# A down-projection with early row splits at its start and a written order on four engines in its second half

## The chip, the cores and the metric

The kernel runs on one core of a Trainium2 chip. The metric is the device time of one execution in microseconds (us). The work of a core is shared by TensorE (PE, the matrix engine), VectorE (DVE), ScalarE (ACT), GpSimd (POOL) and SyncE (SP, which issues the loads and stores). Each engine works through its own list of instructions in a fixed order, and semaphores make an instruction wait for results of other engines.

## The reference, cut to what matters

The program is one transformer-like layer: a mixer with two kinds of recurrent heads, and then a feed-forward part with a 3x3 depthwise convolution. Only the end of the feed-forward part and the final norm are touched here:

```python
def _conv_ffn(h, w_up, conv_w, w_down, rows, cols):
    u = _dwconv2d(h @ w_up, conv_w, rows, cols)
    a, b = jnp.split(u, 2, axis=-1)
    return (jax.nn.silu(a) * b) @ w_down
...
        xl = xl + g2 * _conv_ffn(_modulate(_rmsnorm(xl, norm2_w[l]), sh2, sc2), w_up[l], ffn_conv_w[l],
                                 w_down[l], rows, GRID_W)
...
    return _rmsnorm(xl, final_norm_w)
```

There are 1024 tokens and 1024 model columns; the hidden width D_FF is 2816, which is 22 blocks of 128.

## The kernel before, in words

**Three products for one.** Every matrix product is done on split operands: a float32 array x becomes a rounded part xh (a cast, on ACT) and a rest xl = x - xh (a subtraction, on DVE or POOL), and PE adds up xh*wh, xh*wl and xl*wh. So each operand needs a cast and a subtraction before PE can use it.

**Up-projection (lines 1504 to 1586).** For each of the 22 blocks j, PE makes two column blocks of the hidden layer (j and 22 + j) from `low` (the normalised input, split, in 16 tiles with the tags L0 to L15, two tags for each of the eight blocks k of the model width). ACT starts each convolution with the middle tap, DVE adds the other eight taps (line 1524), each a SCALAR_TENSOR_TENSOR on the result of the one before it. ACT applies silu (L1582), POOL multiplies the two halves (L1586) into the tile G[j]. For the last block, j = 21, the two products are first copied out of PSUM into `src` tiles (L1565), so that the down-projection can have the PSUM.

**Down-projection (lines 1598 to 1667).** It runs in two halves, `dh` = 0 and 1, of 512 output columns. In each half PE goes over the 22 blocks c of the hidden width; one step c is 24 matmuls (8 token tiles t by 3 products, in `mm`, L1609), and the eight 128x512 results fill all of PSUM. `down_ops` (L1533) prepares a step: the cast and rest of the weight row (wh L1554 on ACT, wl L1555 on POOL, in four buffers each), and the cast and rest of G[c] (gh L1556 on ACT, gl L1557 on DVE, or on POOL for c < 3 of the first half). The trace names both tiles of the row `gd`; the one of c = 0 is named gh and gl. The row tiles take over the tags of `low`: step c uses L0 and L1 if c is even, L2 and L3 if odd, so the row of step c + 2 can be made only when PE is done with step c. In the second half the last four blocks (18 to 21, `rest`) are prepared into tiles of their own and are multiplied last, with the token tile as the outer loop, so that the token tiles are finished one after the other.

**Between the halves.** `evac` (L1629) takes the eight results out of PSUM on DVE, times g2. `acc` adds them to the residual y (L1634, DVE) and sums the squares of the new y (L1636, ACT). POOL then multiplies y by the weight of the final norm (L1645). At the end `final` (L1647) makes the factor 1/rms with three small POOL operations, scales the two halves of a token tile (ACT L1652, DVE L1653) and stores the tile with one transfer of 512 KB (SP).

**What sets the order.** Instructions of an engine that is under `manual_schedule` keep the order in which the program issues them. For the other engines a planner at build time simulates the program with its own costs, places an instruction when it finds it ready, and prefers the one that the program issues earlier. Neither order changes at run time: an instruction that waits holds up all behind it on its engine. During the up-projection no engine is under manual order, during the down-projection PE is, and from line 1657 on PE and DVE.

Of the kernel before, what the change touches and what calls it, by code (L numbers as in the profile page):

```python
# [9 lines left out]
F32 = mybir.dt.float32  # L10
F32R = mybir.dt.float32r
I32 = mybir.dt.int32
AF = mybir.ActivationFunctionType
ALU = mybir.AluOpType
# [3 lines left out]
P = 128  # L18
D = 1024
KD = D // P  # L20
T = 1024
# [3 lines left out]
NLT = T // P  # L25
# [43 lines left out]
WARM = 4  # L69
NL = 4  # L70
NGL = 9
MOVE = ((0, 1, 2, 3), (4, 5, 6, 7))


@with_exitstack
def kernel(ctx: ExitStack, tc: tile.TileContext, A: dict, out: bass.AP):
# [15 lines left out]
    def take(units, n):  # L92
        for _ in range(n):
            next(units, None)

    def raw(ap):
        return ap.bitcast(F32)
# [1398 lines left out]
    with ExitStack() as es:  # L1496
        fp = es.enter_context(pool("ff", bufs=2, side="left"))
        f1 = es.enter_context(pool("ff1", bufs=1, side="left"))
        bt = big_tile(2, "bt")
        bcast_cols(g2bc, mod2[:, 3 * KD:4 * KD], (bt[:, 0:512], bt[:, 512:1024]))  # L1500
        fcw = f1.tile([P, 2 * NF, 9], F32, name="fcw")
        SY.dma_start(out=fcw, in_=A["ffcw"].rearrange("p (a b) -> p a b", b=9))

        def up(ct):
            j, b = ct % NF, ct // NF
            if j == 0:
                return early[b][0]
            halves = split_weights(A["wup"][ct])
            pl = big_tile(2 * j + b, "pu")
            for g in range(2):  # L1510
                up_half(pl, halves, g)
            return pl

        def conv2(acc, src, wcol):
            a3 = acc.rearrange("p (r c) -> p r c", c=GW)
            s3 = src.rearrange("p (r c) -> p r c", c=GW)
            S.activation(acc, src, AF.Copy, scale=wcol(4))  # L1517
            for dy in (0, -1, 1):
                for dx in (-1, 0, 1):
                    if dy == 0 and dx == 0:  # L1520
                        continue
                    r0, r1 = max(0, -dy), GH - max(0, dy)
                    c0, c1 = max(0, -dx), GW - max(0, dx)
                    V.scalar_tensor_tensor(  # L1524
                        a3[:, r0:r1, c0:c1], s3[:, r0 + dy:r1 + dy, c0 + dx:c1 + dx],
                        wcol((dy + 1) * 3 + dx + 1), a3[:, r0:r1, c0:c1], op0=ALU.mult, op1=ALU.add)

        pst = {}

        def g_pool(j):  # L1530
            return Gp if j < NGL else Gr

        def down_ops(c, dh, kind):  # L1533
            if c % 2 == 0:
                st = wp.tile([P, 2, 512], F32, name="wst", bufs=3)
                SY.dma_start(out=st, in_=A["wdown"][dh, c // 2].rearrange("p (a b) -> p a b", a=2))
                pst["s"] = st
                if kind == 2:
                    pst["w"] = [g_pool(c - NF + NL + i).tile([P, 2, 512], F32R, name="wd", tag=f"G{c - NF + NL + i}")
                                for i in range(2)]  # L1540
            src = pst["s"][:, c % 2, :]
            if kind == 2:
                wh, wl = [w[:, c % 2, :] for w in pst["w"]]
                gh, gl = [g_pool(j).tile([P, T], F32R, name="gd", tag=f"G{j}")
                          for j in range(NL + 2 * (c - NF + NL), NL + 2 * (c - NF + NL) + 2)]
            else:
                wh = wp.tile([P, 512], F32R, name="wh", bufs=4)
                wl = wp.tile([P, 512], F32R, name="wl", bufs=4)
                if kind:
                    gh, gl = [lo.tile([P, T], F32R, name="gd", tag=f"L{2 * (c % 2) + i}") for i in range(2)]  # L1550
                else:
                    gh = Gr.tile([P, T], F32R, name="gh")
                    gl = Gr.tile([P, T], F32R, name="gl")
            S.copy(wh, src)  # L1554
            G.tensor_tensor(wl, src, raw(wh), op=ALU.subtract)  # L1555
            S.copy(gh, Gt[c])  # L1556
            (G if dh == 0 and c < 3 else V).tensor_tensor(gl, Gt[c], raw(gh), op=ALU.subtract)  # L1557
            return gh, gl, wh, wl

        def up_src(ct, last):  # L1560
            pl = up(ct)
            if not last:
                return pl
            src = fp.tile([P, T], F32, name="src", tag="cb")
            S.copy(src, pl)  # L1565
            return src

        for j in range(NF):
            if j < len(MOVE):
                for k in MOVE[j]:  # L1570
                    SY.dma_start(out=raw(low[0][k]), in_=raw(h2h[k]))
                    SY.dma_start(out=raw(low[1][k]), in_=raw(h2l[k]))
            if j == len(MOVE) + 1:
                h2h[:], h2l[:] = low
                h2_cm.__exit__(None, None, None)
                Gr = ctx.enter_context(pool("Gr", side="right"))
                Gt.extend(Gr.tile([P, T], F32, name=f"G{i}") for i in range(NGL, NF))
            if j == NF - 1:
                pre0 = down_ops(0, 0, 0)
            pl = up_src(j, j == NF - 1)  # L1580
            conv2(Gt[j], pl, lambda i: fcw[:, j, i:i + 1])
            S.activation(Gt[j], Gt[j], AF.Silu)  # L1582
            pl = up_src(NF + j, j == NF - 1)
            cb = fp.tile([P, T], F32, name="cb", tag="cb")
            conv2(cb, pl, lambda i: fcw[:, NF + j, i:i + 1])
            G.tensor_tensor(Gt[j], Gt[j], cb, op=ALU.mult)  # L1586


# [4 lines left out]
    ms_cm = tc.manual_schedule(engines={mybir.EngineType.PE})  # L1593
    ms_cm.__enter__()
    ys = [lo.tile([P, D], F32, name=f"y{t}", tag=f"L{4 + t}") for t in range(NLT)]
    s0 = d1.tile([P, NLT, 2], F32, name="s0")
    pre = [pre0]
    for dh in range(2):
        ds_ = slice(dh * 512, (dh + 1) * 512)
        pp = [big_tile(i, "pd") for i in range(NLT // 2)]  # L1600
# [2 lines left out]
        def part(c, last, dh=dh):  # L1603
            return down_ops(c, dh, 2 if last else 1)

        def mm(t, c, gh, gl, wh, wl):
            ts_ = slice(t * P, (t + 1) * P)
            for pi, (x, w) in enumerate(((gh, wh), (gh, wl), (gl, wh))):
                PE.matmul(po[t], x[:, ts_], w,  # L1609
                          start=(c == 0 and pi == 0), stop=(c == NF - 1 and pi == 2))  # L1610

        n = NF - NL * dh
        for c in range(n):
            if dh == 0 and 6 <= c < 6 + NLT:
                SY.dma_start(out=ys[c - 6], in_=x1d[c - 6])
            ops = pre.pop(0) if pre else part(c, False)
            for t in (0, 4, 1, 5, 2, 6, 3, 7):
                mm(t, c, *ops)
        rest = [part(c, True) for c in range(n, NF)]

        yt = []
# [2 lines left out]
        def evac(t):  # L1624
            if not yt:
                pair = lo.tile([P, T], F32, name="ytmp", tag=f"L{next(slots)}")
                yt.extend((pair[:, 0:512], pair[:, 512:1024]))
            tmp = yt.pop(0)
            V.tensor_tensor(tmp, po[t], g2bc[:, ds_], op=ALU.mult)  # L1629
            return tmp  # L1630

        def acc(t, tmp):
            y = ys[t][:, ds_]
            V.tensor_tensor(y, y, tmp, op=ALU.add)  # L1634
            sq = dn_.tile([P, 512], F32, name="fsq")
            S.activation(sq, y, AF.Square, accum_out=s0[:, t, dh:dh + 1])  # L1636
            return y

        if dh == 0:
            order = (0, 4, 1, 5, 2, 6, 3, 7)  # L1640
            tmps = [evac(t) for t in order]
            pre = [part(c, False, 1) for c in range(2)]
            for t, tmp in zip(order, tmps):
                y = acc(t, tmp)
                G.tensor_tensor(y, y, fnw[:, ds_], op=ALU.mult)  # L1645
            continue
        def final(t, y):  # L1647
            rs = dn_.tile([P, 2], F32, name="rs")
            G.tensor_tensor(rs[:, 0:1], s0[:, t, 0:1], s0[:, t, 1:2], op=ALU.add)
            G.tensor_scalar(rs[:, 0:1], rs[:, 0:1], 1.0 / D, EPS, op0=ALU.mult, op1=ALU.add)  # L1650
            G.tensor_tensor(rs[:, 1:2], rs[:, 0:1], neghalf[:, 0:1], op=ALU.pow)
            S.activation(ys[t][:, 0:512], ys[t][:, 0:512], AF.Copy, scale=rs[:, 1:2])  # L1652
            V.scalar_tensor_tensor(y, y, rs[:, 1:2], fnw[:, ds_], op0=ALU.mult, op1=ALU.mult)  # L1653
            SY.dma_start(out=out[t * P:(t + 1) * P, :], in_=ys[t])

        ms_cm.__exit__(None, None, None)
        ms_cm = tc.manual_schedule(engines={mybir.EngineType.PE, mybir.EngineType.DVE})
        ms_cm.__enter__()
        pend = None
        for t in range(NLT):  # L1660
            for i, ops in enumerate(rest):
# [2 lines left out]
            if pend is not None:  # L1664
                final(*pend)
            pend = cur
        final(*pend)
    ms_cm.__exit__(None, None, None)


# [81 lines left out]
```

## Time and profile before

| what | value |
|---|---|
| three timed runs | 1559.97, 1560.64, 1569.72 us; median 1560.64 us |
| the profiled execution's own time | 1561.63 us |
| its span, first to last instruction | 1559.8 us |
| PE busy | 1491.9 us, 96% of the span |
| DVE busy | 1111.6 us, 71% |
| POOL busy | 597.6 us, 38% |
| ACT busy | 543.4 us, 35% |
| mean granted TensorE clock | 0.990 of full speed |

The profiled execution took 1.83 us more than its span, for what lies before the first and after the last instruction. A busy share alone says little: a matmul counts as busy from its start to a modelled end, and matmuls overlap, so the step from one start to the next is what to read.

### The profile page before, as it was taken

What the parts mean: (1) busy time and instruction counts of PE and PEld (TensorE: products, weight loads), DVE (VectorE), ACT (ScalarE), POOL (GpSimd) and SP (SyncE); (2) the same over time, 40 slices, a digit from 0 to 9 for tenths busy, and PEclk for the clock granted to TensorE, in tenths of its full rate; (3) what the DMA queues carried; (4) which work ended last, traced back from release to release, by engine and by line L of the source; (5) the groups of instructions that cost most, each with busy time, mean ns of one, the idle gap of its engine ahead of it and who ended that gap; (6) DMA issues with size and microseconds to landing.
All of it is one profiled execution on the core that took longest, in us unless ns stands there. A gap on an engine that the chain in (4) does not pass through costs nothing.

```text
span 1559.8 us, 22517 instructions
## 1 busy us (share of the span) xinstructions
PE 1491.9 (96%) x8934; PEld 1213.9 (78%) x8934; DVE 1111.6 (71%) x1460; ACT 543.4 (35%) x950; POOL 597.6 (38%) x510
## 2 busy tenths in 40 slices
PE   7998999998999999999999999999999998998998
PEld 4666788887877777777867888888888886886886
DVE  6957757878396776766578998998989887226334
ACT  4451243344234253433553222222222222323332
POOL 0262144454254654523222433333333335335341
PEclk9999999999999999999999999999999999999999
DMA  9256322112121211135466111111111114111102
GB/s 377 101 183 207 109 78 68 55 54 68 57 84 54 69 46 38 42 101 180 163 219 261 46 49 54 41 55 42 53 55 41 55 41 161 55 41 41 54 27 108
DMA packets 47935, 141.78 MB, mean 91 GB/s; under 512 B 4947, under 2 KB 15059, under 8 KB 47830
## 3 DMA queue, kind: packets, MB, share of 16 engines
q1 hardware_dynamic: 47830, 140.35, 26.5%
q8 instruction: 70, 1.15, 0.3%
q14 instruction: 35, 0.29, 0.1%
HBM read 119.81 MB, written 12.13 MB: 85 GB/s over the span
## 4 chain that ended last, share of the span: by engine, by line
PE 71%; DVE 7%; POOL 2%; ACT 2%; issue 2%; DMA 1%; POOLq 0%; ACTq 0%; DVEq 0%; SPq 0%
PE pu L1463 30%; PE pd L1609 14%; PE po L1319 3%; PE pl_hg L543 3%; PE pl_zb L543 3%; PE pl_zf L543 3%; PE pl_mo L543 2%; PE pl_mq L543 2%; PE pc L543 1%; PE pl_hq L543 1%; PE ap L1122 1%; DVE G L1524 1%; PE pl_mk L543 1%; POOL QQ L1159 1%; DMA g<-gd 1%
## 5 line engine op out<-in xcount | busy, mean ns | idle before, releaser
L1463 PE MATMUL pu<-low,wh 128*128 128x512 f32 x1216 | 374.5, 389 | 0.0
L133 ACT CAST wh<-wst 128x512 fp32r<-128x512 f32 x184 | 112.0, 620 | 528.9 <-issue 227.7
L135 POOL TENSOR_TENSOR wl<-wst,wh 128x512 fp32r<-128x512 f32 x114 | 150.7, 1324 | 356.9 <-ACT wh L133 343.9
L1463 PEld LDWEIGHTS pu<-low,wh 128*128 128x128 f32 x1216 | 228.3, 188 | 47.5
L1463 PE MATMUL pu<-low,wl 128*128 128x512 f32 x608 | 236.5, 389 | 0.0
L1524 DVE SCALAR_TENSOR_TENSOR G<-pu,fcw,G 128x945 f32<-128x945 f32 (+2 forms) x168 | 205.3, 1222 | 24.3 <-ACT G L1517 19.4
L1524 DVE SCALAR_TENSOR_TENSOR cb<-pu,fcw,cb 128x945 f32<-128x945 f32 (+2 forms) x168 | 205.3, 1222 | 23.3 <-ACT cb L1517 18.5
L1609 PE MATMUL pd<-wh,gd 128*128 128x512 f32 x624 | 195.9, 395 | 11.6 <-DVE gd L1557 6.7
L1557 DVE TENSOR_TENSOR gd<-G,gd 128x1024 fp32r<-128x1024 f32 x41 | 56.9, 1389 | 129.9 <-ACT gd L1556 129.8
L1609 PEld LDWEIGHTS pd<-wh,gd 128*128 128x128 f32 x624 | 119.1, 191 | 37.9 <-DVE gd L1557 7.8
L1159 POOL TENSOR_TENSOR QQ<-QQ,FF 128x256 f32<-128x256 f32 x112 | 108.1, 986 | 81.5 <-PE ap L1122 38.2
L1463 PEld LDWEIGHTS pu<-low,wl 128*128 128x128 f32 x608 | 114.2, 188 | 23.6
L1609 PE MATMUL pd<-wl,gd 128*128 128x512 f32 x312 | 123.0, 394 | 0.0
L1555 POOL TENSOR_TENSOR wl<-wst,wh 128x512 fp32r<-128x512 f32 x40 | 73.3, 1835 | 114.0 <-ACT wh L1554 114.0
L135 DVE TENSOR_TENSOR wl<-wst,wh 128x512 fp32r<-128x512 f32 x70 | 57.2, 837 | 57.8 <-ACT wh L133 57.6
L1556 ACT CAST gd<-G 128x1024 fp32r<-128x1024 f32 x43 | 45.0, 1049 | 131.7 <-PE pd L1609 125.0
L1609 PEld LDWEIGHTS pd<-wl,gd 128*128 128x128 f32 x312 | 59.6, 191 | 12.5
L1152 DVE TENSOR_TENSOR KK<-KK,FF 128x768 f32<-128x768 f32 (+1 forms) x56 | 52.1, 941 | 14.9 <-PE tps L1138 11.5
L1586 POOL TENSOR_TENSOR G<-G,cb 128x1024 f32<-128x1024 f32 x22 | 53.9, 2450 | 14.9 <-DVE cb L1524 14.9
L908 POOL TENSOR_SCALAR kw<-ktok,WS 128x128 f32<-128x128 f32 x60 | 24.9, 417 | 49.3 <-PE st L910 49.0
L1115 ACT COPY X<-KK 128x512 f32<-128x512 f32 x40 | 26.9, 681 | 47.0 <-DVE KK L1152 33.9
L341 POOL TENSOR_TENSOR wl<-wst,wh 128x512 fp32r<-128x512 f32 x18 | 31.5, 1766 | 30.4 <-ACT wh L333 21.6
(390 smaller groups left out, 3067.9 us busy)
## 6 DMA issues: line engine op xcount, KB each, us to landing
wst<-in_wup_dram SPq DMA_DIRECT2D x44, 512.0 KB, 3.3
wst<-in_wcm_dram SPq DMA_DIRECT2D x28, 512.0 KB, 3.4
wst<-in_wmod_dram SPq DMA_DIRECT2D x26, 512.0 KB, 3.4
wst<-in_wout_dram SPq DMA_DIRECT2D x24, 512.0 KB, 3.7
wst<-in_wdown_dram SPq DMA_DIRECT2D x22, 512.0 KB, 3.3
wst<-in_wvml_dram SPq DMA_DIRECT2D x10, 512.0 KB, 5.9
x<-in_xcT_dram SPq DMA_DIRECT2D x8, 512.0 KB, 6.5
wsh<-in_wsh_dram SPq DMA_DIRECT2D x8, 512.0 KB, 9.9
```

Of the source, the lines that this page charges most:

```text
L133: S.copy(wh, st[:, hs_])
L135: (eng or G).tensor_tensor(wl, st[:, hs_], raw(wh), op=ALU.subtract)
L543: PE.matmul(o, w[:, ws], x[k][:, c0:c1], start=(k == 0 and pi == 0), stop=(k == KD - 1 and pi == 2))
L1152: V.tensor_tensor(kv, kv, tk, op=ALU.mult)
L1159: G.tensor_tensor(qv, qv, tq, op=ALU.mult)
L1319: PE.matmul(po[g], x[k][:, ts_], halves[g][wi], start=(k == 0 and pi == 0), stop=(k == KD - 1 and pi == 2))
L1463: PE.matmul(pl[:, gs], w[:, ws], x[k][:, gs], start=(k == 0 and pi == 0), stop=(k == KD - 1 and pi == 2))
L1524: V.scalar_tensor_tensor(a3[:, r0:r1, c0:c1], s3[:, r0 + dy:r1 + dy, c0 + dx:c1 + dx], wcol((dy + 1) * 3 + dx + 1), a3[:, r0:r1, c0:c1], o ...
L1555: G.tensor_tensor(wl, src, raw(wh), op=ALU.subtract)
L1557: (G if dh == 0 and c < 3 else V).tensor_tensor(gl, Gt[c], raw(gh), op=ALU.subtract)
L1586: G.tensor_tensor(Gt[j], Gt[j], cb, op=ALU.mult)
L1609: PE.matmul(po[t], x[:, ts_], w, start=(c == 0 and pi == 0), stop=(c == NF - 1 and pi == 2))
```

## The change

There are five edits.

1. **Ring.** The row tiles of the first half use four pairs of tags in turn, (L0, L1), (L2, L3), (L12, L13), (L14, L15), in place of two. The second half keeps two pairs.
2. **Early splits.** At j = 21 the program issues both products of the last block first, then `down_ops` of c = 1, 2 and 3, and only then the two convolutions. Before, only c = 0 stood ahead of them. All rests gl are now on DVE, none on POOL.
3. **Order by hand in the second half.** From the end of the first half on, ACT, DVE and POOL are under manual order as PE is. In that order the row of c = 0 comes ahead of the eight `evac`, and each later step c of PE is followed by the preparation of c + 2, then two of the eight `acc` (c = 0 to 3), then, for c = 4 to 11, one `scaled` unit of POOL (the product with the final norm's weight, and the eps).
4. **Fewer small operations.** The squares are summed with a scale of 1/sqrt(D), and eps is added beforehand, so `final` has two POOL operations ahead of the scaling in place of three.
5. **Last store.** The last token tile is stored as two halves, one issued by ACT and one by SP.

```diff
+RING = ((0, 2, 12, 14), (0, 2))
...
-                    gh, gl = [lo.tile([P, T], F32R, name="gd", tag=f"L{2 * (c % 2) + i}") for i in range(2)]
+                    gh, gl = [lo.tile([P, T], F32R, name="gd", tag=f"L{RING[dh][c % len(RING[dh])] + i}") for i in range(2)]
...
-            (G if dh == 0 and c < 3 else V).tensor_tensor(gl, Gt[c], raw(gh), op=ALU.subtract)
+            V.tensor_tensor(gl, Gt[c], raw(gh), op=ALU.subtract)
...
-            if j == NF - 1:
-                pre0 = down_ops(0, 0, 0)
-            pl = up_src(j, j == NF - 1)
-            conv2(Gt[j], pl, lambda i: fcw[:, j, i:i + 1])
+            if j < NF - 1:
+                pls = [up(j), None]
+            else:
+                pre = [down_ops(0, 0, 0)]
+                pls = [up_src(j), up_src(NF + j)]
+                pre += [down_ops(c, 0, 1) for c in range(1, 4)]
+            conv2(Gt[j], pls[0], lambda i: fcw[:, j, i:i + 1])
             S.activation(Gt[j], Gt[j], AF.Silu)
-            pl = up_src(NF + j, j == NF - 1)
             cb = fp.tile([P, T], F32, name="cb", tag="cb")
-            conv2(cb, pl, lambda i: fcw[:, NF + j, i:i + 1])
+            conv2(cb, pls[1] or up(NF + j), lambda i: fcw[:, NF + j, i:i + 1])
...
             for t in (0, 4, 1, 5, 2, 6, 3, 7):
                 mm(t, c, *ops)
+            if dh and c + 2 < n:
+                pre.append(part(c + 2, False))
+                take(late[0], 2)
+                if c > 3:
+                    take(late[1], 1)
...
-            S.activation(sq, y, AF.Square, accum_out=s0[:, t, dh:dh + 1])
+            S.activation(sq, y, AF.Square, scale=D ** -0.5, accum_out=s0[:, t, dh:dh + 1])
...
+            ms_cm.__exit__(None, None, None)
+            ms_cm = tc.manual_schedule(engines={mybir.EngineType.PE, mybir.EngineType.DVE, mybir.EngineType.Activation,
+                                                mybir.EngineType.Pool})
+            ms_cm.__enter__()
+            pre = [part(0, False, 1)]
             tmps = [evac(t) for t in order]
-            pre = [part(c, False, 1) for c in range(2)]
-            for t, tmp in zip(order, tmps):
-                y = acc(t, tmp)
-                G.tensor_tensor(y, y, fnw[:, ds_], op=ALU.mult)
+            pre.append(part(1, False, 1))
+
+            def sums(todo, acc=acc):
+                for t, tmp in todo:
+                    acc(t, tmp)
+                    yield
+
+            def scaled(fs=fnw[:, ds_]):
+                for t in order:
+                    y = ys[t][:, 0:512]
+                    G.tensor_scalar(s0[:, t, 0:1], s0[:, t, 0:1], 1.0, EPS, op0=ALU.mult, op1=ALU.add)
+                    G.tensor_tensor(y, y, fs, op=ALU.mult)
+                    yield
+
+            late = (sums(list(zip(order, tmps))), scaled())
             continue
...
+        def final(t, y, one=True):
+            G.tensor_tensor(s0[:, t, 3:4], s0[:, t, 0:1], s0[:, t, 1:2], op=ALU.add)
+            rs = dn_.tile([P, 1], F32, name="rs")
+            G.tensor_tensor(rs, s0[:, t, 3:4], neghalf[:, 0:1], op=ALU.pow)
+            S.activation(ys[t][:, 0:512], ys[t][:, 0:512], AF.Copy, scale=rs)
+            if not one:
+                S.dma_start(out=out[t * P:(t + 1) * P, 0:512], in_=ys[t][:, 0:512])
+            V.scalar_tensor_tensor(y, y, rs, fnw[:, ds_], op0=ALU.mult, op1=ALU.mult)
+            if one:
+                SY.dma_start(out=out[t * P:(t + 1) * P, :], in_=ys[t])
+            else:
+                SY.dma_start(out=out[t * P:(t + 1) * P, 512:1024], in_=y)
...
-        final(*pend)
+        final(*pend, False)
```

## Rows read from the trace of the kernel before

**Rows 1.** The page: its head, and of its fourth part (the chain of work that ended last) the shares by engine.

```profile
span 1559.8 us, 22517 instructions
...
PE 71%; DVE 7%; POOL 2%; ACT 2%; issue 2%; DMA 1%; POOLq 0%; ACTq 0%; DVEq 0%; SPq 0%
```

**Rows 2.** Busy time by stretch: the stretch, its length, then busy time and count of PE, PEld, DVE, ACT and POOL, the granted TensorE clock (1.00 is 2.4 GHz, 0.50 is 1.2 GHz), the DMA share and GB/s. Stretches around the two gaps of PE in the down-projection.

```profile
1312.50:1318.70 6.20, 0.00 (x1) 0.00 (x1) 6.06 (x7) 0.92 (x2) 0.00 (x0) 0.77 0.26 85
1318.70:1322.70 4.00, 4.00 (x10) 3.15 (x11) 2.19 (x2) 0.00 (x0) 2.87 (x1) 0.51 0.00 0
...
1434.60:1439.50 4.90, 0.02 (x1) 0.00 (x0) 3.12 (x3) 2.99 (x8) 4.90 (x4) 0.92 0.00 0
1439.50:1445.50 6.00, 5.52 (x12) 3.98 (x13) 3.86 (x2) 1.94 (x3) 6.00 (x4) 0.50 0.00 0
```

**Rows 3.** Busy time by stretch of the down-projection's matmuls alone (L1609): the stretch, its length, PE, PEld, clock, DMA share, GB/s. Each stretch holds one step c of 24 matmuls (the counts take in those that reach over an edge): c = 3 and c = 4 of the first half, c = 2 and c = 3 of the second.

```profile
1311.80:1325.60 13.80, 7.60 (x26) 5.80 (x25) 0.75 0.23 72
1325.60:1331.04 5.44, 5.44 (x25) 4.50 (x25) 1.00 0.21 62
...
1434.44:1448.30 13.86, 8.50 (x25) 6.26 (x25) 0.75 0.11 35
1448.30:1453.74 5.44, 5.44 (x25) 4.50 (x24) 1.00 0.02 6
```

**Rows 4.** Waits of PE from 1250 us to the end: all of them. Columns: us in total, times, the longest.

```profile
PE pd L1609 <- DVE gd L1557: 6.7, 2, 6.2
PE pd L1609 <- ACT gd L1556: 4.9, 1, 4.9
```

**Rows 5.** Timeline of DVE at the change to the down-projection: start, length, operation, count, and in brackets the idle time before it and what ended it.

```profile
1287.30 17.30 DVE L1524 SCALAR_TENSOR_TENSOR G<-src,fcw,G 128x1008 f32<-128x1008 f32 x8 [1.87 <-ACT G L1517]
1306.89 10.62 DVE L1524 SCALAR_TENSOR_TENSOR cb<-src,fcw,cb 128x1008 f32<-128x1008 f32 x7 [2.29 <-ACT cb L1517]
1317.42 1.22 DVE L1557 TENSOR_TENSOR gd<-G,gd 128x1024 fp32r<-128x1024 f32 x1
1318.56 1.20 DVE L1524 SCALAR_TENSOR_TENSOR cb<-src,fcw,cb 128x945 f32<-128x945 f32 x1
1319.67 1.22 DVE L1557 TENSOR_TENSOR gd<-G,gd 128x1024 fp32r<-128x1024 f32 x1
```

**Rows 6.** The same stretch: three rows of POOL's timeline, and of the chain that ended last two single convolution taps (start, length).

```profile
1286.50 2.39 POOL L1586 TENSOR_TENSOR G<-G,cb 128x1024 f32<-128x1024 f32 x1
1291.97 6.07 POOL L1557 TENSOR_TENSOR gd<-G,gd 128x1024 fp32r<-128x1024 f32 x2 [3.08 <-ACT gd L1556]
1298.01 4.34 POOL L1555 TENSOR_TENSOR wl<-wst,wh 128x512 fp32r<-128x512 f32 x2
...
1292.54 3.24 DVE G L1524
...
1303.40 1.21 DVE G L1524
```

**Rows 7.** Timeline of ACT in the same stretch.

```profile
1290.84 2.00 ACT L1556 CAST gd<-G 128x1024 fp32r<-128x1024 f32 x2 [3.57 <-PE pu L1463]
...
1295.96 1.01 ACT L1565 COPY src<-pu 128x1024 f32<-128x1024 f32 x1
...
1307.21 1.05 ACT L1556 CAST gd<-G 128x1024 fp32r<-128x1024 f32 x1
```

**Rows 8.** Timelines of ACT, DVE and POOL at the change from the first half to the second.

```profile
1437.80 0.63 ACT L1636 ACTIVATE fsq<-y 128x512 f32<-128x512 f32 x1 [0.95 <-DVE y L1634]
...
1438.43 1.03 ACT L1556 CAST gd<-G 128x1024 fp32r<-128x1024 f32 x1
...
1420.34 4.87 DVE L1629 TENSOR_TENSOR ytmp<-pd,g2bc 128x512 f32<-128x512 f32 x8
...
1426.26 11.45 DVE L1634 TENSOR_TENSOR y<-y,ytmp 128x512 f32<-128x512 f32 x8
1439.49 3.87 DVE L1557 TENSOR_TENSOR gd<-G,gd 128x1024 fp32r<-128x1024 f32 x2 [1.78 <-ACT gd L1556]
...
1428.87 13.41 POOL L1645 TENSOR_TENSOR y<-y,fnw 128x512 f32<-128x512 f32 x8 [1.39 <-ACT fsq L1636]
```

**Rows 9.** A later step of the second half, where no engine is late: ACT, DVE, POOL.

```profile
1459.18 1.05 ACT L1556 CAST gd<-G 128x1024 fp32r<-128x1024 f32 x1 [3.87 <-PE pd L1609]
1460.13 0.62 ACT L1554 CAST wh<-wst 128x512 fp32r<-128x512 f32 x1
...
1460.27 1.22 DVE L1557 TENSOR_TENSOR gd<-G,gd 128x1024 fp32r<-128x1024 f32 x1 [1.98 <-ACT gd L1556]
...
1460.83 1.81 POOL L1555 TENSOR_TENSOR wl<-wst,wh 128x512 fp32r<-128x512 f32 x1 [3.63 <-ACT wh L1554]
```

**Rows 10.** The end: ACT's scaling of the last token tile but one, one small POOL operation, the last scaling on DVE; then the stretch in which the packets of the last store move (columns as in Rows 2), and the stores as a group (count, KB each, median us from issue to landing).

```profile
1552.80 0.72 ACT L1652 ACTIVATE y<-y,rs 128x512 f32<-128x512 f32 x1 [1.21 <-POOL rs L1651]
...
1554.69 0.19 POOL L1650 TENSOR_SCALAR rs<-rs 128x1 f32<-128x1 f32 x1
...
1555.55 0.75 DVE L1653 SCALAR_TENSOR_TENSOR y<-y,rs,fnw 128x512 f32<-128x512 f32 x1 [1.37 <-POOL rs L1651]
...
1557.20:1558.60 1.40, 0.00 (x0) 0.00 (x0) 0.00 (x0) 0.00 (x0) 0.00 (x0) 0.50 0.91 375
...
out_dram<-y SPq DMA_DIRECT2D x8, 512.0 KB, 2.6
```

More of the change, by code (lines that the diff above doesn't have):

```diff
@@ L1556, in down_ops, with up_src @@
             S.copy(gh, Gt[c])
-            (G if dh == 0 and c < 3 else V).tensor_tensor(gl, Gt[c], raw(gh), op=ALU.subtract)
+            V.tensor_tensor(gl, Gt[c], raw(gh), op=ALU.subtract)
             return gh, gl, wh, wl
-        def up_src(ct, last):
+        def up_src(ct):
             pl = up(ct)
-            if not last:
-                return pl
             src = fp.tile([P, T], F32, name="src", tag="cb")
@@ L1595 @@
     ys = [lo.tile([P, D], F32, name=f"y{t}", tag=f"L{4 + t}") for t in range(NLT)]
-    s0 = d1.tile([P, NLT, 2], F32, name="s0")
-    pre = [pre0]
+    s0 = d1.tile([P, NLT, 4], F32, name="s0")
     for dh in range(2):
@@ L1630, in evac, with acc @@
             return tmp
-        def acc(t, tmp):
+        def acc(t, tmp, dh=dh, ds_=ds_):
             y = ys[t][:, ds_]
@@ L1640 @@
             order = (0, 4, 1, 5, 2, 6, 3, 7)
-            tmps = [evac(t) for t in order]
-            pre = [part(c, False, 1) for c in range(2)]
-            for t, tmp in zip(order, tmps):
-                y = acc(t, tmp)
-                G.tensor_tensor(y, y, fnw[:, ds_], op=ALU.mult)
-            continue
[L1647 to L1654, printed above, removed]
@@ L1656 @@
-        ms_cm.__exit__(None, None, None)
-        ms_cm = tc.manual_schedule(engines={mybir.EngineType.PE, mybir.EngineType.DVE})
-        ms_cm.__enter__()
+            ms_cm.__exit__(None, None, None)
[3 more added lines that the diff above has]
+            pre = [part(0, False, 1)]
+            tmps = [evac(t) for t in order]
```

## The prediction, made before the changed kernel was run

> **What bounds the kernel now.** I read the page first: PE holds 71% of the chain that ended last, the next engine 7% [rows 1]. So a gain has to come from time in which PE stands still or runs slowly. The change touches nothing ahead of the last block of the up-projection, so I looked at the down-projection alone.
>
> A step of 24 matmuls takes 5.44 us when nothing is late. Two steps don't: c = 3 of the first half takes 13.80 us, c = 2 of the second 13.86 us [rows 3]. Their excess is 8.36 and 8.42 us, together **16.78 us**. The waits of PE say why: 6.2 us for a `gd` of DVE in the first case, 4.9 for one of ACT and the rest of 6.7 (0.5) for one of DVE in the second, and none else [rows 4]. The remainder, 8.36 - 6.20 = 2.16 and 8.42 - 5.36 = 3.06 us, is the clock: it fell while PE waited, and after each wait PE ran 4.0 and 6.0 us at 0.51 and 0.50 of full speed, the 1.2 GHz level, before it was back at 2.4 GHz [rows 2].
>
> **Why they are late.** *First gap.* Step c = 3 uses the tags of c = 1, so its cast could start only when PE was done with c = 1; ACT made it at 1307.21 [rows 7]. Its rest on DVE then stood behind seven taps of the last convolution and ran at 1317.42, one tap before the end [rows 5]. The convolution itself was slow: eight taps of block 21 took 17.30 us [rows 5], against 8 x 1.21 = 9.7 by a free tap [rows 6]. POOL was at work in 12.0 us of that stretch (1.6 of the product that began at 1286.50, two rests of 6.07, two of 4.34); a tap in the middle of it took 3.24 [rows 6]. The 7.6 us lost are 0.63 us for each us of POOL. *Second gap.* The cast for c = 2 stood behind the eight sums of squares on ACT, the last at 1437.80, and began at 1438.43; each sum waited for an addition on DVE, and the eight took 11.45 us, since POOL's 13.41 us of norm products ran beside them [rows 8]. PE had been free to hand over the tags at about 1429, 5.44 us ahead of the gap.
>
> **The change, part by part.**
>
> *Ring and early splits.* The rows of c = 1 to 3 go to tags that the last up-projection product frees, not PE's down steps. L2/L3 come free where the first cast now stands, 1290.84 [rows 7], and L12 to L15 within the last 1.4 us of that product (two of its eight k, 3 matmuls each, 6 x 0.227), so by about 1295.5 (1311.8 less three steps). Three casts of 1.05 [rows 7], three rests of 1.22 [rows 5]: the last, with the copy of `src` at 1295.96 ahead of it on ACT [rows 7], is made near 1301. PE reaches c = 3 at 1311.8 [rows 3] and, in steps of 5.44 back from there, c = 2 at 1306.4 and c = 1 at 1300.9. Even with taps of 3.24 between them, the rest of c = 1 is made by 1295 and that of c = 3 by 1303. So c = 3 is on time by some 9 us, and the question moves to **c = 4**, due at 1311.8 + 5.44 = 1317.2; its rest is read first by the third matmul, 0.45 later. It uses L0/L1, free before L2/L3, so its cast can be made near 1291 to 1299. Its place on DVE is the planner's. Before, the planner put a rest between two taps as soon as it found it ready (1317.42, ahead of the last tap [rows 5]), and DVE has a hole of 2.29 us ahead of the second convolution [rows 5]. I take it that the rest of c = 4 lands there or earlier, some 10 us ahead of need. From then on four pairs of tags keep rows three steps ahead. DVE gets two rests more (2.4 us) and POOL's overlap falls; the convolution ends about where it did, and its result is needed only at c = 21. The extra rest of c = 0 falls in the middle of the up-projection, where DVE waits for PE once a half block. Gain: 8.36, cover as named; lower bound in the first rival.
>
> *Order by hand.* Per step PE releases two tags, ACT casts (1.05), DVE subtracts (1.22) [rows 9]: 2.3 to 2.4 us, and PE wants the result 5.44 us after the release. On ACT the new order puts ahead of the cast one wh and the two squares of the step before; on DVE two additions. All of them are ready some 2 us before the release: additions right after the previous rest, 2 x 0.7, the squares another 1.6. wl (1.81 [rows 9]) has a step more. The norm products leave the additions alone, since they come from c = 4 on; each adds about 1.7 us (13.41 / 8 [rows 8]) to POOL's 1.81 in a step of 5.44. The eight evacuations began at 1420.34, behind a rest of DVE, and took 4.87 [rows 8]; the order keeps that pattern, and the rest for c = 1 follows them at about 2.4 us into a step of which it has 5.44. The last four blocks were prepared early before; now they queue behind the cast of c = 17, which waits for PE's c = 15. ACT then needs 1.05 + 4 x (1.05 + 0.62) [rows 9], DVE 1.2 behind that, so all is there 8.9 us later; POOL's four wl, at up to 1.81, end at about the same time. PE comes there after two steps, 10.88. Slack 2 us, and more for the later blocks. Gain: 8.42.
>
> *Fewer POOL operations.* One of 0.19 and its gap leave the tail: from 1554.69 to the next start, 0.28 us [rows 10].
>
> *Tail order and the last store.* ACT's scaling of the last tile but one ran at 1552.80, ahead of the last square [rows 10]. By hand it stands behind the square, and its store starts 0.7 us later. The packets of a store move for 1.40 us at 375 GB/s [rows 10]. Old: that store was done before the last began; new: about 0.35 us of it is left when the last one starts, 0.28 earlier. So the tail gains between 0.28 and -0.3; with no row for a store issued by ACT, I take SP's 2.6 us to landing [rows 10] for both halves, and the tail at **0**. If two halves on two queues moved side by side, half of the 1.40 would be saved, which is the far end (-0.7). The Trainium skill (DMA: Bandwidth & Descriptors, section Issuing engines are not separate DMA queues) says that transfers of all issuing engines share the same 16 DMA engines, so that only issue time is saved; by it the split gives 0 and the tail stands as taken. The row with a DMA share of 0.91 for one store [rows 10] agrees.
>
> **Sum.** 1561.63 (profiled) - 8.36 - 8.42 - 0 = 1544.85. The median of the timed runs lies 0.99 below the profiled one, so on that footing **1543.9**; I say 1544. A measurement of this kernel can tell about 1%, 15.6 us, so the line for faster is 1545.0: the forecast lies just beyond it.
>
> **Rivals.**
>
> *c = 4 late* (0.12). If the planner puts its rest behind all taps: taps 16 x 1.21 = 19.4, hole 2.29, three rests 3.7, POOL overlap (1.6 of the product, four wl of 1.81) 8.8 x 0.63 = 5.6; from 1287.30 that is 1318.3, with the rest 1319.5, 1.8 us after need (1317.7). With the clock's 2.2 at worst: 1545.7 to 1547.9. For it: the program issues it later. Against it: [rows 5] as above. The Trainium skill (SBUF — State Buffer, section Who interferes with whom) calls the port pair of DVE and POOL an exclusive lock held for a whole instruction; by it all 8.8 us would be lost, and this rival would cost up to 7.1 and end at 1551. The 0.63 measured here lies below that.
>
> *The second half waits a little* (0.08): the four last blocks or a square in front of a cast come 1 to 3 us late, with the clock up to 3.1 more: 1545 to 1550. For it: slack of only 2 us; against: it grows with each block.
>
> *The opening doesn't change* (0.06): no manual order holds there, so the planner may still lay the early rests behind the taps. Only the second gap closes: 1543.9 + 8.4 = 1552.3. Against it: POOL's two rests of c = 1 and 2 were placed early [rows 6] from a later place in the program.
>
> *Slower* (0.04): in the four steps with sums, cast and rest get stuck behind squares and additions. At worst in series: cast 1.05, wh 0.62 [rows 9], a slowed rest 3.87 / 2 = 1.9, two squares 1.3, two slow additions 2 x 11.45 / 8 = 2.9 [rows 8]: 7.8, so 2.3 us beyond 5.44 in each; the clock adds 2.2 to 3.1 each time: 18 to 22 us. It decides once the waits cost more than the 16.8 gained, 4.2 per step, and ends at 1562 to 1566. Against it: the order issues them behind the cast, not ahead.
>
> **How the numbers follow.** Forecast 0.70; its own range 1542.8 to 1546 (0.3 and 0.7 of the tail, 1 us of small waits). Beyond it up to 1552.5 lie the first two rivals and half of the third, which leaves out about 0.13. Faster by over 1%: 0.70 x 0.8, since the line lies 1 us above the forecast, plus 0.03 of the first rivals, 0.59. Slower 0.04. Same 0.37.
>
> **What would show it.** Right: no wait of PE over 0.3 us in the down-projection, clock 1.00 from the last up-projection matmul to the end, 44 steps of 5.44; three rests on DVE among the first taps and one in the hole; the cast for c = 2 of the second half 5 us ahead of PE, squares after it. Wrong: a wait of PE on `gd` at c = 4, or at the first of the last four blocks, or on `wl` in the second half.

## The result, and the profile after

The changed kernel takes 1544.47 us (median of 4 runs, 1542.36 to 1545.79), the kernel before 1562.12 us (4 runs). The ratio is 0.9877 with a 95% interval of 0.9841 to 0.9913: **1.2% faster**, with 0.9% and 1.6% as the bounds. The forecast was 1544.0.

The head of the page and the chain's shares by engine, beside [rows 1]: the span is 16.6 us shorter, and PE holds 73% of the chain in place of 71%.

```profile
span 1543.2 us, 22515 instructions
...
PE 73%; DVE 5%; POOL 3%; issue 3%; ACT 2%; DMA 1%; POOLq 0%; SPq 0%; ACTq 0%; DVEq 0%
```

The view of PE's waits from 1250 us to the end, which had two rows before [rows 4], has none. The down-projection's matmuls by stretch (stretch, its length, PE, PEld, clock, DMA share, GB/s), the same four steps as in [rows 3]: c = 3 and 4 of the first half, c = 2 and 3 of the second. Those that took 13.80 and 13.86 us now take 5.44.

```profile
1311.95:1317.39 5.44, 5.44 (x26) 4.50 (x25) 1.00 0.31 96
1317.39:1322.83 5.44, 5.44 (x26) 4.51 (x25) 1.00 0.00 0
1426.19:1431.63 5.44, 5.44 (x26) 4.51 (x25) 1.00 0.32 96
1431.63:1437.07 5.44, 5.44 (x26) 4.50 (x25) 1.00 0.00 0
```

Busy time of all engines around both changes (columns as in [rows 2]): PE is busy in the whole of each stretch and its granted clock is 1.00, the 2.4 GHz level, where it was at 0.51 and 0.50 after the waits.

```profile
1295.00:1345.00 50.00, 50.00 (x222) 41.27 (x221) 32.76 (x23) 17.38 (x22) 20.15 (x11) 1.00 0.38 134
1395.00:1434.00 39.00, 39.00 (x173) 32.29 (x172) 14.19 (x19) 10.83 (x19) 9.85 (x6) 1.00 0.13 41
1434.00:1480.00 46.00, 46.00 (x204) 38.11 (x203) 12.24 (x13) 15.74 (x25) 27.25 (x25) 1.00 0.14 48
```

The opening, casts on ACT (columns as in [rows 7]) and rests on DVE (as in [rows 5]). The pair of casts at 1291.02 is c = 4 and c = 1, the two after it c = 2 and c = 3; the cast at 1308.30 is c = 5. On DVE the pair at 1293.87 is c = 4 and c = 1, then c = 2, and c = 3, done at 1305.1.

```profile
1291.02 2.01 ACT L1557 CAST gd<-G 128x1024 fp32r<-128x1024 f32 x2 [3.57 <-PE pu L1464]
...
1295.10 1.05 ACT L1557 CAST gd<-G 128x1024 fp32r<-128x1024 f32 x1 [1.55 <-PE pu L1464]
...
1297.48 1.05 ACT L1557 CAST gd<-G 128x1024 fp32r<-128x1024 f32 x1
...
1308.30 1.04 ACT L1557 CAST gd<-G 128x1024 fp32r<-128x1024 f32 x1
```

```profile
1287.49 6.47 DVE L1525 SCALAR_TENSOR_TENSOR G<-src,fcw,G 128x1008 f32<-128x1008 f32 x4 [1.88 <-ACT G L1518]
1293.87 3.45 DVE L1558 TENSOR_TENSOR gd<-G,gd 128x1024 fp32r<-128x1024 f32 x2
...
1300.52 1.21 DVE L1558 TENSOR_TENSOR gd<-G,gd 128x1024 fp32r<-128x1024 f32 x1
...
1302.78 2.31 DVE L1558 TENSOR_TENSOR gd<-G,gd 128x1024 fp32r<-128x1024 f32 x1
```

The change of halves (beside [rows 8]): on ACT the cast for c = 2 stands at 1420.84, ahead of all squares; on DVE two additions take 1.28 us in place of eight in 11.45.

```profile
1420.84 1.05 ACT L1557 CAST gd<-G 128x1024 fp32r<-128x1024 f32 x1 [3.87 <-PE pd L1609]
1423.78 0.63 ACT L1641 ACTIVATE fsq<-y 128x512 f32<-128x512 f32 x1 [1.89 <-DVE y L1639]
```

```profile
1423.07 1.28 DVE L1639 TENSOR_TENSOR y<-y,ytmp 128x512 f32<-128x512 f32 x2
```

### The profile page after: what moved, and what is told of

The parts are those of the page before. It is cut to its first block, busy times and chain, and to the rows that moved or that the text cites. A ratio compares the mean times of both kernels' runs of the same rounds, so it can differ in the third digit from the quotient of the medians.

```text
span 1543.2 us, 22515 instructions
## 1 busy us (share of the span) xinstructions
PE 1487.6 (96%) x8934; PEld 1211.2 (78%) x8934; DVE 1101.0 (71%) x1463; ACT 542.7 (35%) x950; POOL 586.8 (38%) x507
## 4 chain that ended last, share of the span: by engine, by line
PE 73%; DVE 5%; POOL 3%; issue 3%; ACT 2%; DMA 1%; POOLq 0%; SPq 0%; ACTq 0%; DVEq 0%
PE pu L1464 31%; PE pd L1609 14%; PE po L1320 3%; PE pl_hg L544 3%; PE pl_zb L544 3%; PE pl_zf L544 3%; PE pl_mo L544 2%; PE pl_mq L544 2%; PE pc L544 1%; PE pl_hq L544 1%; PE ap L1123 1%; PE pl_mk L544 1%; DMA g<-gd 1%; POOL QQ L1160 1%; PE st L911 1%
## 5 line engine op out<-in xcount | busy, mean ns | idle before, releaser
L136 POOL TENSOR_TENSOR wl<-wst,wh 128x512 fp32r<-128x512 f32 x114 | 150.8, 1325 | 357.5 <-ACT wh L134 341.8
L1609 PE MATMUL pd<-wh,gd 128*128 128x512 f32 x624 | 192.4, 389 | 0.0
L1558 DVE TENSOR_TENSOR gd<-G,gd 128x1024 fp32r<-128x1024 f32 x43 | 60.3, 1409 | 130.9 <-ACT gd L1557 130.9
L1609 PEld LDWEIGHTS pd<-wh,gd 128*128 128x128 f32 x624 | 117.2, 188 | 24.3
L1609 PE MATMUL pd<-wl,gd 128*128 128x512 f32 x312 | 121.4, 389 | 0.0
L1556 POOL TENSOR_TENSOR wl<-wst,wh 128x512 fp32r<-128x512 f32 x40 | 69.0, 1726 | 128.7 <-ACT wh L1555 128.7
L1609 PEld LDWEIGHTS pd<-wl,gd 128*128 128x128 f32 x312 | 58.6, 188 | 12.1
L342 POOL TENSOR_TENSOR wl<-wst,wh 128x512 fp32r<-128x512 f32 x18 | 31.6, 1774 | 30.3 <-ACT wh L334 21.5
```

What stands on the lines that cost most here:

```text
L136: (eng or G).tensor_tensor(wl, st[:, hs_], raw(wh), op=ALU.subtract)
L1558: V.tensor_tensor(gl, Gt[c], raw(gh), op=ALU.subtract)
L1609: PE.matmul(po[t], x[:, ts_], w, start=(c == 0 and pi == 0), stop=(c == NF - 1 and pi == 2))
```

## The experiments

**How they are compared.** Single spans mislead here. Up to the last block of the up-projection the program is the same in all of these kernels but for one subtraction (the rest of c = 0, on POOL or on DVE), yet the first matmul of the down-projection started anywhere from 1293.24 to 1300.70 us. So I compare the stretch from that matmul to the end of the span; for the kernel before the two numbers come from this row and [rows 1], for the one after from the second row and its page. Each stretch is one profiled execution, and the last seven kernels were also timed only once. The edits are shown against the changed kernel, cut to what matters ("...").

```profile
1295.41 0.39 PE L1609 MATMUL pd<-wh,gh 128*128 128x512 f32 x1
```

```profile
1295.59 0.39 PE L1609 MATMUL pd<-wh,gh 128*128 128x512 f32 x1
```

| kernel | first matmul | span | stretch | over the changed kernel |
|---|---|---|---|---|
| before | 1295.41 | 1559.8 | 264.4 | +16.8 |
| after | 1295.59 | 1543.2 | 247.6 | 0 |
| e1_opening_alone | 1293.43 | 1550.1 | 256.7 | +9.1 |
| e2_second_half_alone | 1293.24 | 1549.8 | 256.6 | +9.0 |
| e3_early_two_pairs | 1294.22 | 1545.8 | 251.6 | +4.0 |
| e4_four_pairs_old_issue | 1295.13 | 1542.7 | 247.6 | 0 |
| e5_rests_on_pool | 1300.46 | 1548.3 | 247.8 | +0.2 |
| e6_sums_first | 1295.97 | 1543.5 | 247.5 | -0.1 |
| e7_old_order_by_hand | 1300.70 | 1563.1 | 262.4 | +14.8 |
| e8_old_order_norm_later | 1297.52 | 1547.4 | 249.9 | +2.3 |
| e9_last_store_whole | 1296.42 | 1544.0 | 247.6 | 0 |
| e10_planner_new_issue | 1298.48 | 1546.4 | 247.9 | +0.3 |
| e11_scale_first | 1298.74 | 1546.2 | 247.5 | -0.1 |

My theory was that of the prediction: two gaps, each with its own cause, and nothing else. The rivals were that the gaps hang together, that one edit of each group does all, and that the written order as such is what helps.

**Opening alone.** Edits 1 and 2; the second half and the tail as before.

```diff
...
-            ms_cm = tc.manual_schedule(engines={mybir.EngineType.PE, mybir.EngineType.DVE, mybir.EngineType.Activation,
-                                                mybir.EngineType.Pool})
...
-            pre = [part(0, False, 1)]
             tmps = [evac(t) for t in order]
-            pre.append(part(1, False, 1))
+            pre = [part(c, False, 1) for c in range(2)]
...
```

> Edits 1 and 2 alone; the second half stays as before. Two-gap theory: only the first gap goes, so the kernel before less 8.4 us, about 1552.5; PE waits for no gd at c = 3, and still waits about 5.4 us at c = 2 of the second half. Rival (the written order does all of it, since without it the planner lays the rests late): about as before, 1560 to 1562, with a wait at c = 3 or c = 4 of the first half.

Measured: 1552.54 us, ratio 0.9938 (0.9915 to 0.9960). The waits of PE (columns as in [rows 4]) are those of the second gap alone:

```profile
PE pd L1609 <- ACT gd L1557: 4.9, 1, 4.9
PE pd L1609 <- DVE gd L1558: 0.7, 1, 0.7
```

**Second half alone.** Edits 3 to 5; ring and issue order of the opening as before.

```diff
-RING = ((0, 2, 12, 14), (0, 2))
+RING = ((0, 2), (0, 2))
...
-            V.tensor_tensor(gl, Gt[c], raw(gh), op=ALU.subtract)
+            (G if dh == 0 and c < 3 else V).tensor_tensor(gl, Gt[c], raw(gh), op=ALU.subtract)
...
```

> Edits 3 to 5 alone; the opening of the down-projection stays as before. Two-gap theory: only the second gap goes, the kernel before less 8.4 us, about 1552.5, with the wait of 6.2 us at c = 3 kept. Rival (the gaps are coupled, the second comes from the delay of the first): less than 3 us of gain or the whole 16.8.

Measured: 1552.98 us, ratio 0.9939 (0.9922 to 0.9956), and only the wait of the first gap:

```profile
PE pd L1609 <- DVE gd L1558: 6.2, 1, 6.2
```

Gains of 0.62 and 0.61%, each within about 0.2, add up to the whole change's 1.23%: the gaps are independent, and neither edit moves its wait elsewhere. (By the stretches they are 7.7 and 7.8 of 16.8 us; the last section says where the remainder lies.)

**Early issue without the ring.**

```diff
-RING = ((0, 2, 12, 14), (0, 2))
+RING = ((0, 2), (0, 2))
```

> The changed kernel with two pairs of tags in place of four, the early issue kept. If the ring carries the gain, the cast for c = 3 waits for PE's c = 1 until about 1306.6 and is made near 1308.3; its rest lands near 1314, against a need at 1312.5, and c = 4 follows the same way: waits of 2 to 4 us in all, 2 to 6 us above the changed kernel, that is 1546.5 to 1550.5. If the early issue (and the rests taken off POOL) carries it, no wait and 1544.5. If neither does without the other, the whole 8.4 us come back: 1553.

Measured: 1548.91 us, ratio 0.9918 (0.9896 to 0.9940). One wait is left, and the cast of c = 3 shows whose: on ACT it starts at 1305.23, released by PE's c = 1, and the rest stands behind five taps on DVE. The three fences show PE's waits, ACT and DVE.

```profile
PE pd L1609 <- DVE gd L1558: 2.1, 1, 2.1
```

```profile
1305.23 1.06 ACT L1557 CAST gd<-G 128x1024 fp32r<-128x1024 f32 x1 [0.71 <-PE pd L1609]
```

```profile
1304.10 8.13 DVE L1525 SCALAR_TENSOR_TENSOR cb<-src,fcw,cb 128x1008 f32<-128x1008 f32 x5 [2.28 <-ACT cb L1518]
1312.15 1.22 DVE L1558 TENSOR_TENSOR gd<-G,gd 128x1024 fp32r<-128x1024 f32 x1
```

So with two pairs the early issue, with the rests on DVE, takes away about half of the first gap, and 4.0 us of it stay.

**The ring without the early issue.** Four pairs, rests on DVE, but the program issues only c = 0 ahead of the convolutions, as before.

```diff
...
-                pre = [down_ops(0, 0, 0)]
-                pls = [up_src(j), up_src(NF + j)]
-                pre += [down_ops(c, 0, 1) for c in range(1, 4)]
-            conv2(Gt[j], pls[0], lambda i: fcw[:, j, i:i + 1])
+                pre = [down_ops(0, 0, 0)]
+            pl = up_src(j, j == NF - 1)
+            conv2(Gt[j], pl, lambda i: fcw[:, j, i:i + 1])
...
```

> The changed kernel with four pairs of tags, but with the preparation of c = 1 to 3 issued after the convolutions, as before. The planner places what it finds ready, so the ring alone should do: 1544.5, no wait of PE. Rival (the place in the program decides): the rests stand behind the taps, c = 1 to 3 come at 1318 or later, and PE waits up to 16 us from c = 1 on: 1555 to 1565.

Measured: 1543.9 us, ratio 0.9884 (0.9864 to 0.9904), no wait. The planner puts the casts where they were with the early issue, to within half a microsecond:

```profile
1290.56 2.01 ACT L1557 CAST gd<-G 128x1024 fp32r<-128x1024 f32 x2 [3.57 <-PE pu L1464]
...
1294.64 1.05 ACT L1557 CAST gd<-G 128x1024 fp32r<-128x1024 f32 x1 [1.55 <-PE pu L1464]
...
1297.02 1.05 ACT L1557 CAST gd<-G 128x1024 fp32r<-128x1024 f32 x1
```

So with the rests on DVE the ring needs no early issue: it carries the whole gain of the opening.

**Rests of c = 0 to 2 back on POOL.**

```diff
-            V.tensor_tensor(gl, Gt[c], raw(gh), op=ALU.subtract)
+            (G if dh == 0 and c < 3 else V).tensor_tensor(gl, Gt[c], raw(gh), op=ALU.subtract)
```

> The changed kernel with the rests gl of c = 0 to 2 on POOL again, all else kept. If the gain of the opening comes from the tags alone, PE still waits for nothing, and the span is the changed kernel's 1543.2 within 0.5; DVE's taps of block 21 take longer (up to 17 us for eight, as before). If taking the rests off POOL was needed, PE waits 1 us or more at c = 3 to 5.

Measured: 1550.1 us, no wait of PE. The span misses the expectation by 5 us, but all of that lies ahead of the down-projection, which started 4.9 us later; the stretch is 247.8. DVE and POOL do slow each other (a rest of 3.42 us on DVE beside one of 3.09 on POOL), and with four pairs nothing waits for it: POOL made the rest of c = 2 by 1306.6 and PE reads it at about 1311.8, by steps of 5.44 from its start. So with the ring and the early issue, moving the rests off POOL was not needed. The ring by itself, with the old issue order and the rests on POOL, was not run.

```profile
1298.73 3.42 DVE L1558 TENSOR_TENSOR gd<-G,gd 128x1024 fp32r<-128x1024 f32 x1
```

```profile
1297.98 3.09 POOL L1558 TENSOR_TENSOR gd<-G,gd 128x1024 fp32r<-128x1024 f32 x1 [4.03 <-PE pu L1464]
```

**Sums ahead of the cast, in the written order.**

```diff
             if dh and c + 2 < n:
-                pre.append(part(c + 2, False))
                 take(late[0], 2)
+                pre.append(part(c + 2, False))
```

> The changed kernel with the two sums of each step issued ahead of the preparation of c + 2, not behind it. My theory: they are ready before PE hands over the tags, so they fill time in which ACT and DVE wait: no wait of PE, span 1543.2 within 0.3. The rival on the slower side (a cast that is stuck behind squares) gives waits of 1 to 2.3 us in each of four steps, 4 us or more.

Measured: 1545.33 us, stretch 247.5, no wait. Two additions and two squares fit in the slack of a step on either side of the cast.

**The old order, written by hand.** Four engines under manual order, but the instructions in the program order of before: eight evacuations, rows of c = 0 and 1, then all eight additions, squares and norm products.

```diff
-            if dh and c + 2 < n:
-                pre.append(part(c + 2, False))
-                take(late[0], 2)
...
-            pre = [part(0, False, 1)]
             tmps = [evac(t) for t in order]
-            pre.append(part(1, False, 1))
+            pre = [part(c, False, 1) for c in range(2)]
...
+            for t in order:
+                take(late[0], 1)
+                take(late[1], 1)
```

> The changed kernel with all four engines under manual order in the second half, but in the order in which the kernel before issued its work: evacuations, preparation of c = 0 and 1, then all eight sums with the norm products between, then each step's preparation when PE comes to it. If the order is what counts, the second gap is back: a wait of about 5 us at c = 2 and 8 us in all, span about 1551.5. If manual order as such helps, no wait, 1543.2.

Measured: 1564.85 us, stretch +14.8: worse than I expected, and the waits are others than before.

```profile
PE pd L1609 <- POOL wl L1556: 9.4, 1, 9.4
PE pd L1609 <- DVE gd L1558: 2.1, 1, 2.1
```

On POOL the `wl` of c = 2 stood behind the eight norm products; the planner of before had run it at 1425.20, ahead of them.

```profile
1441.07 1.26 POOL L1657 TENSOR_TENSOR y<-y,fnw 128x512 f32<-128x512 f32 x1
1442.29 3.73 POOL L1556 TENSOR_TENSOR wl<-wst,wh 128x512 fp32r<-128x512 f32 x3
```

A fixed order as such gives nothing; a wrong one costs as much as the right one gains.

**The same, with the norm products later** (one in each of c = 4 to 11, as the change has them).

```diff
+            if dh and c > 3:
+                take(late[1], 1)
...
-            for t in order:
-                take(late[0], 1)
-                take(late[1], 1)
+            take(late[0], 8)
```

> As the run before, but POOL's norm products come in steps c = 4 to 11. If POOL's work beside the additions is the larger cause, the eight additions take about 5 us in place of 11.45, the squares end about 9 us after the first half and the wait at c = 2 is under 1 us: span 1543.2 to 1545. If the place of the cast behind eight sums is enough by itself, the wait stays 3 us or more: span 1548 to 1552.

Measured: 1549.22 us, stretch +2.3. PE no longer waits at c = 2, though ACT still works through all eight squares ahead of that cast. With POOL away, eight additions on DVE take 4.90 us; with its norm products beside them they took 7.11 in the run before this one, and 11.45 in [rows 8].

```profile
1421.02 4.90 DVE L1636 TENSOR_TENSOR y<-y,ytmp 128x512 f32<-128x512 f32 x8
```

That came with little to spare. PE was 2.2 us late already, for the wait at c = 0 below. The rest of c = 2 was done at 1429.76; PE read it at 1431.04, and would have wanted it at about 1428.7 without that delay:

```profile
1428.29 1.47 DVE L1558 TENSOR_TENSOR gd<-G,gd 128x1024 fp32r<-128x1024 f32 x1 [2.37 <-ACT gd L1557]
```

So this run does not show that the cast behind eight squares would be in time for a PE that is not late. What is left is one wait at c = 0, whose rest stands behind the eight evacuations:

```profile
PE pd L1609 <- DVE gd L1558: 2.1, 1, 2.1
```

So against the hand-written old order, moving POOL's norm products is worth 12.5 us of the stretch (`wl` no longer stands behind them, and the additions run free), and the last 2.3 go with the wait at c = 0, which the change avoids by its row ahead of the evacuations.

**New issue order, planner on ACT, DVE and POOL** up to the last four blocks.

```diff
-            ms_cm.__exit__(None, None, None)
-            ms_cm = tc.manual_schedule(engines={mybir.EngineType.PE, mybir.EngineType.DVE, mybir.EngineType.Activation,
-                                                mybir.EngineType.Pool})
-            ms_cm.__enter__()
             pre = [part(0, False, 1)]
...
```

> The changed kernel with its new issue order, but with ACT, DVE and POOL left to the planner from the end of the first half to the last four blocks. If the written order is needed, the planner lays the sums and POOL's norm products together as soon as it finds them ready, the additions slow down again, and PE waits 2 to 6 us at c = 2: the down-projection loses 3 to 8.5 us. If the issue order alone does it, no wait and a loss of 0.4.

Measured: 1548.13 us, no wait listed, stretch +0.3; the start was 2.9 us later. The waits that I gave for a needed written order did not come. The planner lays the eight additions and squares together again, with POOL's norm products beside them (seven additions take 7.59 us on DVE), but from the new place of the row in the program it puts the cast of c = 2 among the squares, at 1424.70, just in time: its rest is done at 1429.72, and PE reads it at 1429.78, where by steps of 0.227 it would have read it at 1429.65. The changed kernel has that rest at 1423.15 (1.23 us from 1421.92), some 3.4 us ahead of its reading. The rows of DVE, ACT and PE:

```profile
1421.00 7.59 DVE L1639 TENSOR_TENSOR y<-y,ytmp 128x512 f32<-128x512 f32 x7
1428.51 1.21 DVE L1558 TENSOR_TENSOR gd<-G,gd 128x1024 fp32r<-128x1024 f32 x1
```

```profile
1424.07 0.63 ACT L1641 ACTIVATE fsq<-y 128x512 f32<-128x512 f32 x1
...
1424.70 1.04 ACT L1557 CAST gd<-G 128x1024 fp32r<-128x1024 f32 x1
```

```profile
1429.78 0.73 PE L1609 MATMUL pd<-wh,gd 128*128 128x512 f32 x2
```

**Last store whole**, and **scaling ahead of the next square** (tail only).

```diff
-        final(*pend, False)
+        final(*pend)
```

> The changed kernel with the last token tile stored by one transfer of 512 KB from SP, as before. The stretch from the start of the last matmul to the end of the span is 8.08 us with two halves. If the two halves share the same engines and save nothing, it stays at 8.0 to 8.2. If halving saves transfer time, it becomes 8.5 to 8.8.

```diff
...
-            cur = (t, acc(t, evac(t)))
+            tmp = evac(t)
+            rs = scale(pend[0]) if pend is not None else None
+            y = acc(t, tmp)
             if pend is not None:
-                final(*pend)
-            pend = cur
+                store(*pend, rs)
+            pend = (t, y)
...
```

> The changed kernel with ACT's scaling of each finished token tile issued ahead of the square of the next, as the planner placed it before, so that the store of the last tile but one starts 0.7 us earlier. If the two last stores stand in each other's way, the stretch from the last matmul to the end falls from 8.08 to about 7.8 (the 0.28 us of the POOL operation then show). If not, 8.08; if the scaling now delays the last square, 8.3 or more.

Measured: 1545.73 and 1547.94 us. From the start of the last matmul to the end of the span the changed kernel takes 8.08 us (before: 8.17), the whole store 8.04, the scaling first 7.93. Halving the store saves nothing; the other order saves 0.15, half of what I expected and far below what a time can tell. The POOL operation that is gone was not run by itself; the scaling first, 7.93 against 8.17 before, is 0.24 shorter, near the 0.28 that the prediction gave it.

## Why the prediction was right

**What bounds it: right.** All of the gain is the excess of the two steps: 16.8 us by the stretches of the table, against 16.78 forecast. The clock's part came back with the waits, as the sum had it, and 44 steps of 5.44 and the tail of 8.08 account for the stretch to half a microsecond. That the median too lies within 0.5 us of the forecast is in part luck: the start of the down-projection alone varies by 7.5 us between profiled runs, with all of it in the time.

**Ring and early splits: right in size, the credit too wide.** The three rests and c = 4's were on time. I had c = 1 made by 1295 and c = 3 by 1303; they were made at 1297.3 and 1305.1, because the cast of c = 4 went first, and its rest with c = 1's, and rests ran slowed (3.45 us for the first pair, 2.31 for c = 3, where one takes 1.21 alone), but PE reached them at 1301.0 and 1311.9. (The first cast waits for the first k of the product, so what comes free there is L0/L1; L2/L3 follow one k, 3 x 0.227 = 0.7 us, later than I had it, without effect.) The question of c = 4 never arose: its rest was made by 1297.3 at the latest, 20 us ahead of need (1317.4), not in the hole ahead of the second convolution. So the condition of that rival, a rest behind all taps, did not come near. What I did not see is that the ring needed neither the early issue (with the rests on DVE) nor the rests on DVE (with the early issue); no run leaves out both.

**Order by hand: right in effect, half right in cause.** I named the cast behind the squares and POOL's products beside the additions together. The runs set them apart: with either undone, PE no longer waited at c = 2. With the norm products later the cast stood behind eight squares, though for a PE that came 2.2 us late; with the norm products early a cast among the squares was in time, and that the planner does by itself from the new issue order, to 0.3 us. So the written order is not needed for the gain; what it buys is slack, 3.4 us at c = 2 where the planner's order had none.

**The last four blocks: mis-sized, without harm.** I had them all there 8.9 us after the release of c = 17, with 2 us of slack. The release came at 1502.43, the last rest was done at 1513.69, so 11.3 us. Four rests on DVE and four `wl` on POOL ran together:

```profile
1504.99 8.70 DVE L1558 TENSOR_TENSOR gd<-G,gd 128x1024 fp32r<-128x1024 f32 x4 [0.25 <-ACT gd L1557]
```

```profile
1504.08 8.53 POOL L1556 TENSOR_TENSOR wd<-wst,wd 128x512 fp32r<-128x512 f32 x4 [3.63 <-ACT wd L1555]
```

That is 2.18 and 2.13 us each, where one takes 1.22 and 1.29 alone; I had slowed POOL only, to 1.81. PE reached the four blocks at 1513.34, before the last was ready. It did not wait because the token tile is the outer loop there: each block takes three matmuls, so the fourth block's rest is first read after 11 of them, 1513.34 + 11 x 0.227 = 1515.8, which leaves 2.1 us. The Trainium skill (SBUF — State Buffer, section Who interferes with whom) says that a DVE instruction with two SBUF inputs contends with a GpSimd instruction that reads SBUF, over a port pair held exclusively. One after the other the eight would take 4 x 1.22 + 4 x 1.29 = 10.0 us; from the first start to the last end they took 9.6 (1504.08 to 1513.69), so here the trace nearly agrees with the lock. Undisturbed they would have taken about 6.5, an estimate: ACT's last cast ended at 1509.37, and one rest of 1.22 follows it. My sum took no loss on DVE here, though I had one of 0.63 us per us of POOL from the convolution; here it was 8.70 - 4 x 1.22 = 3.8 us beside 8.53 of POOL, 0.45.

**Tail: right.** Taken at 0, measured 0.09 us. The scaling of the last tile but one stands behind the square now, and the two halves of the last store are issued at 1539.44 by ACT and 1539.46 by SP:

```profile
1537.03 0.63 ACT L1641 ACTIVATE fsq<-y 128x512 f32<-128x512 f32 x1 [1.41 <-DVE y L1639]
...
1537.66 0.71 ACT L1673 ACTIVATE y<-y,rs 128x512 f32<-128x512 f32 x1
...
1539.44 0.40 ACTq L1675 DMA_DIRECT2D out_dram<-y  x1
```

The whole store took no longer (8.04 against 8.08), so the rule that the prediction weighed (the Trainium skill, DMA: Bandwidth & Descriptors, section Issuing engines are not separate DMA queues) stands in this case, and the far end of -0.7 falls.

**The chances.** The slower rival needs a loss in each of four steps; all lost nothing, since the squares came behind the cast and two additions took 1.28 us, and a run with the sums ahead of the cast lost nothing either.

## What to carry to other kernels

Where PE waits for prepared operands, first count the buffers: a ring with two more pairs took the whole gap with the old issue order, while issuing the work earlier into the old buffers took half (the rests were on DVE in both). Where two engines slow each other, ask which of the two has time: with POOL's products a few steps later PE no longer waited at c = 2, where the waits of the kernel before named DVE and ACT. A listing without waits does not tell how much slack there is: look at when the operand was done and when it was read. Compare runs from a common instruction on when the work ahead of it varies by more than the effect.

## What was not expected of the hardware

- **The same wait has different prices.** A wait of 2.1 us cost 4.0 us in the early issue with two pairs, and 2.3 us with the norm products later. In the first the clock fell behind it, to a mean of 0.73 over 6.3 us; in the second it stayed at 1.00. Both waits came after PE had run at 1.00; what decides it no run here shows. The two rows, in that order (columns as in [rows 2]):

```profile
1313.30:1319.60 6.30, 6.18 (x20) 4.95 (x21) 4.74 (x5) 0.00 (x0) 2.55 (x1) 0.73 0.00 0
```

```profile
1419.80:1425.00 5.20, 4.97 (x22) 4.13 (x23) 5.20 (x9) 3.26 (x11) 0.00 (x0) 1.00 0.01 3
```

- **So has the same gap.** Each gap alone left a little more than its share: 9.1 and 9.0 us, of which 5.6 and 6.2 were waits, so 3.5 and 2.8 us besides, where the kernel before had 3.06 and 2.16. That too was not traced to a cause.
- **The same instructions start 7.5 us apart.** The first matmul of the down-projection varies from 1293.24 to 1300.70 us in these profiled runs. All of it lies ahead of the up-projection's matmuls on `low`: from the first of them to the first of the down-projection it is 413.4 to 413.5 us in all thirteen kernels. The two extremes (second half alone, old order by hand; count, ns, first and last start):

```profile
L1464 PE MATMUL pu<-low,wh x1216: 389/389/397, 879.8 to 1292.8; 128*128 128x512 f32 x174
L1464 PE MATMUL pu<-low,wh x1216: 389/389/397, 887.2 to 1300.2; 128*128 128x512 f32 x174
```

Where ahead of that the time goes was not followed up.
